# Queries of the cross attention as two 2x2x2 block products in seven multiplications

## The chip, the cores and the metric

The kernel runs on one core of a Trainium2 chip. The core has five engines, each with its own queue of instructions that it works through in order: TensorE (PE, matmuls and transposes; its weight loads are listed apart as PEld), VectorE (DVE), ScalarE (ACT), GpSimd (POOL) and SyncE (SP, which here only starts transfers). POOL starts the transfers that add to their destination ("accumulates"). Transfers between HBM (the `DRAM` of the code) and SBUF run beside the engines. The metric is the device time of one execution in microseconds (us). Three runs of the kernel before took 748.03 to 748.14 us, with a median of 748.14 us.

## The reference

One layer works on 512 tokens of width 1024. In its middle stands a cross attention with 4 heads of 256 onto 256 memory tokens:

```python
h = h + jnp.concatenate([fox_out, rec], axis=-1) @ w_out[l]
mem_n = rmsnorm(mem, norm_mem_g[l])
h = h + memory_cross_attention(rmsnorm(h, norm_x_g[l]), mem_n, w_xq[l], w_xkv[l], w_xo[l])
u = rmsnorm(h, norm_ff_g[l]) @ w1[l]
h = h + jnp.square(jax.nn.relu(u)) @ w2[l]

def memory_cross_attention(h, mem_n, w_q, w_kv, w_o):
    q = (h @ w_q).reshape(b_, s_, X_HEADS, X_HEAD_DIM)
    k, v = jnp.split(mem_n @ w_kv, 2, axis=-1)       # then split into heads
    s = jnp.einsum('bshd,bmhd->bhsm', q, k).astype(jnp.float32) / math.sqrt(X_HEAD_DIM)
    p = jax.nn.softmax(s, axis=-1)
    o = jnp.einsum('bhsm,bmhd->bshd', p.astype(v.dtype), v).reshape(b_, s_, D_MODEL)
    return o @ w_o
```

Before it stand an input projection, forgetting attention ("fox") and a gated recurrence; behind it the MLP with w1 and w2 and a final norm. All is in float32. The change concerns `q = h @ w_q`, a product of 512x1024 by 1024x1024.

## The kernel before

**Arithmetic.** A float32 product is made of three matmuls with operands of a reduced float32 type (`fp32r`): each operand is split into a high part and the rest, and hi*hi, lo*hi and hi*lo are summed in PSUM. For weights, ACT makes the high part (`wh..`, L184) and DVE the rest (`wl..`, L188), 128x1024 elements at a time. For activations, `x_hi` is made by ACT and `x_lo` by DVE.

**Stages around the change**, in the order of PE. The product with w_out (`wo`, `residual`, order k 4 to 7 and then 0 to 3) ends with, for each of eight row blocks, the sum into the residual `hT` (L1317, DVE), `x_hi` (L1318, ACT), `x_lo` (L1319, DVE) and two POOL instructions that sum squares (`wosq`, `ssq`). Then `x_proj(0)` makes the queries of head 0: one panel of w_xq, 256 columns in two loads of 512 KB, 48 matmuls of 128x512. The mean of squares (`pm`, `mean_sq`) and the reciprocal root on POOL follow. Then a loop over four heads: `x_scores` for two halves of the tokens (24 matmuls of 128x256 a head) and the softmax (maximum on DVE, exponential on ACT, division on DVE), `x_T_` (transposes `xpt`), the split of the transposed weights (`pth` on ACT, `ptl` on DVE) and `x_out` (12 matmuls of 128x512 a head, `xo`), whose results are split into `o_hi` and `o_lo`. Between these steps PE gets filling work from a list `fill`, in the amounts X1 to X4: beside head h the queries of head h+1, and beside head 3 the beginning of the product with w_xo (`xw`, `residual(...).early`). The rest of `xw` and the MLP come after.

**The weights' stream.** `specs` lists the panels in the order of their use, `next_panel` keeps two panels ahead: it starts the loads on SP and places the splits on ACT and DVE into the program, in its order. Where a split stands in an engine's queue is fixed when the program is built.

**The MLP's seven products.** The MLP is already computed by 2x2 blocks with seven block products in place of eight; matmuls are 128x256 there. It needs sums of weight blocks, which are made in DRAM: SP copies a block (L499) and POOL accumulates another one on it (L509). `Presum` gives one POOL accumulate to the program whenever PE has been given a certain amount of work (`PACE`: from 178 us on, one in 4.7 us, from 301 us on one in 11.5 us). One of the seven weights, "4" of the MLP, is made in SBUF: POOL accumulates a block onto the raw sum of another after that one has been split (L1528).

Of the kernel before, what the change touches and what calls it, by code (L numbers as in the profile page):

```python
# [9 lines left out]
F32 = mybir.dt.float32  # L10
# [6 lines left out]
P = 128  # L17
S = 512
# [28 lines left out]
def emit(  # L47
# [55 lines left out]
    def q2(name):  # L103
        return q2p.tile([P, S], R, tag="q2", name=name)
# [12 lines left out]
    def mm(name, shape=(S,)):  # L117
        return mmp.tile([P] + list(shape), F32, tag="mm", name=name)
# [43 lines left out]
    LATE = len(specs)  # L162
    for j in range(4):
        specs.append(panel(w_xkv, j * WT))
    for w in (w_out, w_xq, w_xo):
        for j in range(4):
            specs.append(panel(w, j * WT))
    NG = DFF // HG
    stream = []
    state = {"used": 0, "halves": 0}  # L170
# [93 lines left out]
    def product_unit(name):  # L264
# [24 lines left out]
            jobs.append(lambda: load_block("5", "10", raw0["5"]))  # L289
        return jobs  # L290

    def next_panel():
        while len(stream) < min(state["used"] + 2, len(specs)):
# [15 lines left out]
    def gemm_fm(ps, wt, col, ahi, alo, n=S, order=range(KC), begun=False):  # L309

        whi, wlo = wt
        sl = slice(col, col + P)
        for n_, k in enumerate(order):
            hi, lo = chunk(ahi, k, slice(0, n)), chunk(alo, k, slice(0, n))
            wh, wl = chunk(whi, k, sl), chunk(wlo, k, sl)
            te.matmul(ps, wh, hi, start=n_ == 0 and not begun, stop=False)  # L316
            te.matmul(ps, wh, lo, start=False, stop=False)  # L317
            at = te.matmul(ps, wl, hi, start=False, stop=k == order[-1])  # L318
            yield presum.tick(3 * n / 2400, at)
# [166 lines left out]
    def block2(g, rc):  # L486
        r, c = int(rc[0]), int(rc[1])
        k0 = g * HG + r * 2 * P
        return w2[k0 : k0 + 2 * P, c * S : (c + 1) * S].rearrange("(k p) n -> p k n", p=P)

    wsum = {}

    def sum_jobs(kind, g):
        block, shape = (block1, [P, UK, WT]) if kind == "u" else (block2, [P, 2, S])
        for name in SUMS:
            wsum[kind, g, name] = drp.tile(shape, F32, name=f"ws{kind}{g}{name}")

        def first(name):
            dma = nc.sync.dma_start(wsum[kind, g, name], block(g, SUMS[name][0]))  # L499
            copied.add((kind, g, name))  # L500
            return dma

        def sums():
            for name, (_, b) in SUMS.items():
                while (kind, g, name) not in copied:
                    copies.popleft()()
# [33 lines left out]
            return us  # L540

    presum = Presum()
    sets = []
    for g in range(DFF // HG):
        if g + 1 in SEVEN:
            sets.append(sum_jobs("u", g + 1))
# [744 lines left out]
    def residual(src_hi, src_lo, g, dst_hi, dst_lo, name, ssq, order, nlast, after=None, hooks={}, open_end=False):  # L1291

        ps_, gens = {}, {}

        def open_(c):
            if c % 2 == 0:
                open_.wt = next_panel()
            ps_[c] = mm(f"{name}{c}")
            gens[c] = gemm_fm(ps_[c], open_.wt, (c % 2) * P, src_hi, src_lo, order=order)

        def early():

            for c in range(3):
                open_(c)
                for _ in range(KC - nlast):
                    yield next(gens[c])

        def rest():
            for c in range(KC):
                if c not in gens:  # L1310
                    open_(c)
                yield from gens[c]
                if open_end and c == KC - 1:
                    last_xw.append(ps_[c])
                    return
                hc = hTc(c)
                ve.tensor_tensor(hc, hc, ps_[c], ALU.add)  # L1317
                ac.activation(dst_hi[:, c, :], hc, AF.Identity, scale=g[:, c : c + 1])  # L1318
                ve.scalar_tensor_tensor(dst_lo[:, c, :], hc, g[:, c : c + 1], f(dst_hi[:, c, :]), op0=ALU.mult, op1=ALU.subtract)  # L1319
# [12 lines left out]

        return early, rest
# [9 lines left out]

    x1_hi, x1_lo = act_tile("x1_hi"), act_tile("x1_lo")
    ssq1 = t2("ssq1")
    _, wo_rest = residual(mx_hi, mx_lo, g_x, x1_hi, x1_lo, "wo", ssq1, (4, 5, 6, 7, 0, 1, 2, 3), 1)
    run_now(wo_rest())


    o_hi, o_lo = act_tile("o_hi"), act_tile("o_lo")  # L1350
    x2 = []
    xq, xps, xpr, xpT = {}, {}, {}, {}

    def x_proj(h):
        wt = next_panel()
        xq[h] = []
        for i in range(2):
            ps = mm(f"xq{h}{i}")
            yield from gemm_fm(ps, wt, i * P, x1_hi, x1_lo)
            a, b = q2(f"xqh{h}{i}"), q2(f"xql{h}{i}")  # L1360
            ac.activation(a, ps, AF.Copy)
            ve.tensor_tensor(b, ps, f(a), ALU.subtract)
            xq[h].append((a, b))

    run_now(x_proj(0))
    ms1 = mean_sq(ssq1, "pm1")
    r1 = rstd_of(ms1, NT, "r1")
    gp.tensor_scalar(r16, r1, 1.0 / 16.0, 0.0, op0=ALU.mult, op1=ALU.add)

    def x_scores(h, tp):  # L1370
        ps = sc(f"xs{h}{tp}", (2, M))
        for j in range(2):
            ts_ = slice((2 * tp + j) * P, (2 * tp + j + 1) * P)
            for i in range(2):
                a, b = xq[h][i]
                kh_, kl_ = kTh[h][:, i, :], kTl[h][:, i, :]
                te.matmul(ps[:, j, :], a[:, ts_], kh_, start=i == 0, stop=False)
                te.matmul(ps[:, j, :], a[:, ts_], kl_, start=False, stop=False)
                te.matmul(ps[:, j, :], b[:, ts_], kh_, start=False, stop=i == 1)
# [12 lines left out]
        xpr[h, tp] = pr_  # L1392
# [38 lines left out]
                ve.tensor_copy(d, s_)  # L1431

    first_hooks, last_xw = {}, []
    fill.add(x_proj(1), "xq1")
    fill.run(2.0)
    for h in range(4):
        if 0 < h < 3:
            fill.add(x_proj(h + 1), f"xq{h + 1}")
        elif h == 3:
            x2_hi, x2_lo = act_tile("x2_hi"), act_tile("x2_lo")  # L1440
            early, rest = residual(o_hi, o_lo, g_ff, x2_hi, x2_lo, "xw", None, range(KC), 2, to_tok, first_hooks, True)
            fill.add(early())
        x_scores(h, 0)
        fill.run(X1)
        x_scores(h, 1)
        fill.run(X2 + X3)
        x_T_(h, 0)
        x_T_(h, 1)
        pth, ptl = s4([2, S], f"pth{h}", R), s4([2, S], f"ptl{h}", R)
        for mc in range(2):  # L1450
            ac.activation(pth[:, mc, :], xpT[h][mc], AF.Copy)
            ve.tensor_tensor(ptl[:, mc, :], xpT[h][mc], f(pth[:, mc, :]), ALU.subtract)
# [604 lines left out]
```

## Time and profile before

| | |
|---|---|
| median of three runs (range) | 748.14 us (748.03 to 748.14) |
| profiled execution, its own time | 748.24 us |
| span of the trace | 746.5 us |
| PE busy | 738.6 us (99%) |
| DVE, ACT, POOL busy | 566.6, 460.4, 213.4 us |
| product with w_out | 264.9 to 308.5 us of the span |
| cross attention from the first query matmul to the last of w_xo | 308.5 to 425.5 us |

Times in the trace count from the start of the span; what lies outside the span is 1.7 us. A row of a timeline has start, duration, engine, line and operation, output<-inputs; in brackets the idle time before it and what ended it. A matmul row's duration is modelled and overlaps the next one; what a matmul costs in a stream is the distance between two starts. Lines are those of the kernel before.

### The profile page before, as it was taken

To read this page: it belongs to the slowest core of one execution; us is meant where nothing else is said; L and a number is where in the kernel's file an instruction comes from. 1 tells how busy PE (TensorE), PEld (TensorE's weight loads), DVE (VectorE), ACT (ScalarE), POOL (GpSimd) and SP (SyncE) were. 2 spreads that over 40 slices of the span, in tenths; PEclk is the share of its full clock that TensorE was granted. 3 is DMA by queue.
4 is the path that set the end of the run, shared out by engine and by line. 5 is a ranking of instruction groups with operands and counts; after the bars stand their busy time and mean duration, and the time that the engine had idled before them with its cause. 6 is when DMAs were issued, how large, how long until landed. Compare 5 with 4: busy or idle time off the path is not lost.

```text
span 746.5 us, 12316 instructions
## 1 busy us (share of the span) xinstructions
PE 738.6 (99%) x4557; PEld 645.3 (86%) x4557; DVE 566.6 (76%) x892; ACT 460.4 (62%) x769; POOL 213.4 (29%) x290
## 2 busy tenths in 40 slices
PE   9999999999999999999999999999999999999996
PEld 6889888898888888888888899898989898999985
DVE  5878997677787866655546898978787878878796
ACT  5875876666666733244435589666665757574864
POOL 7216842442342246621012111111111111100034
PEclk9999999999999999999999999999999999999999
DMA  7797999857955899976669799898989899978352
GB/s 245 217 245 199 259 306 315 279 169 229 336 170 186 274 221 195 213 151 133 125 155 209 117 241 233 243 247 220 241 220 236 209 246 227 234 192 247 120 112 114
DMA packets 111918, 159.22 MB, mean 213 GB/s; under 512 B 6337, under 2 KB 74218, under 8 KB 111858
## 3 DMA queue, kind: packets, MB, share of 16 engines
q1 hardware_dynamic: 85490, 114.62, 46.6%
q0 software_dynamic: 26208, 43.54, 33.0%
q8 instruction: 36, 0.59, 0.3%
q10 hardware_dynamic: 160, 0.27, 0.1%
q14 instruction: 24, 0.20, 0.1%
HBM read 153.15 MB, written 51.40 MB: 274 GB/s over the span
## 4 chain that ended last, share of the span: by engine, by line
PE 90%; DMA 3%; DVE 2%; ACT 2%; issue 1%; POOL 0%; POOLq 0%; DVEq 0%; SPq 0%; ACTq 0%
PE uU L1632 4%; PE uU L1634 4%; PE uU L1633 4%; PE U L1790 3%; PE U L1791 3%; PE U L1792 3%; PE uY L1634 2%; PE uY L1633 2%; PE uY L1632 2%; PE xk L1146 2%; PE xq L316 2%; PE wo L316 2%; PE xq L317 2%; PE xq L318 2%; PE xw L318 2%; PE xw L317 2%
## 5 line engine op out<-in xcount | busy, mean ns | idle before, releaser
L188 DVE TENSOR_TENSOR wlu<-wru,whu 128x1024 fp32r<-128x1024 f32 x53 | 63.9, 1219 | 25.9 <-ACT whu L184 25.9
L184 ACT ACTIVATE whu<-wru 128x1024 fp32r<-128x1024 f32 x53 | 55.9, 1059 | 40.7 <-PE U L1792 16.8
L188 DVE TENSOR_TENSOR wld<-wrd,whd 128x1024 fp32r<-128x1024 f32 x56 | 68.2, 1220 | 13.9 <-ACT whd L184 13.7
L184 ACT ACTIVATE whd<-wrd 128x1024 fp32r<-128x1024 f32 x56 | 59.0, 1054 | 15.3 <-PE uU L1633 6.6
L1790 PE MATMUL U<-whd,hb 128*128 128x512 f32 x120 | 46.8, 390 | 0.0
L1791 PE MATMUL U<-wld,hb 128*128 128x512 f32 x120 | 46.8, 390 | 0.0
L1792 PE MATMUL U<-whd,hb 128*128 128x512 f32 x120 | 46.7, 389 | 0.0
L509 POOL DMA_DIRECT2D wsd<-in_w_dram x16 | 17.8, 1114 | 68.2 <-PE xw L318 16.6
L1167 POOL TENSOR_SCALAR bi<-nF,Ft 128x128 f32<-128x128 f32 (+3 forms) x32 | 20.8, 659 | 56.2 <-PE pt L1203 30.4
L1632 PE MATMUL uU<-xs_hi,whu 128*128 128x256 f32 x128 | 36.3, 284 | 0.0
L1634 PE MATMUL uU<-x_hi,wlu 128*128 128x256 f32 x128 | 36.2, 283 | 0.0
L1632 PE MATMUL uY<-xs_hi,whu 128*128 128x256 f32 x128 | 36.2, 283 | 0.0
L1633 PE MATMUL uY<-xs_lo,whu 128*128 128x256 f32 x128 | 36.2, 283 | 0.0
L1634 PE MATMUL uY<-xs_hi,wlu 128*128 128x256 f32 x128 | 36.2, 283 | 0.0
L1634 PE MATMUL uU<-xs_hi,wlu 128*128 128x256 f32 x128 | 36.2, 283 | 0.0
L1633 PE MATMUL uU<-x_lo,whu 128*128 128x256 f32 x128 | 36.2, 283 | 0.0
L1633 PE MATMUL uU<-xs_lo,whu 128*128 128x256 f32 x128 | 36.2, 283 | 0.0
L1632 PE MATMUL uU<-x_hi,whu 128*128 128x256 f32 x128 | 36.2, 283 | 0.0
L1528 POOL DMA_DIRECT2D wrd<-in_w_dram x8 | 9.8, 1223 | 86.6 <-DVE wld L188 51.4
L509 POOL DMA_DIRECT2D wsu<-in_w_dram x14 | 17.0, 1211 | 44.3 <-PE xq L318 14.5
L1318 ACT ACTIVATE x_hi<-hT,gv 128x512 fp32r<-128x512 f32 x15 | 10.7, 714 | 25.8 <-DVE hT L1317 25.8
L1792 PEld LDWEIGHTS U<-whd,hb 128*128 128x128 f32 x120 | 22.5, 188 | 4.7
(1012 smaller groups left out, 2656.4 us busy)
## 6 DMA issues: line engine op xcount, KB each, us to landing
wru<-in_w_dram SPq DMA_DIRECT2D x25, 512.0 KB, 6.7
wsd<-in_w_dram SPq DMA_DIRECT2D x24, 512.0 KB, 6.9
wrd<-in_w_dram SPq DMA_DIRECT2D x24, 512.0 KB, 4.2
wrd<-wsd SPq DMA_DIRECT2D x24, 512.0 KB, 5.7
wsu<-in_w_dram SPq DMA_DIRECT2D x21, 512.0 KB, 7.2
wru<-wsu SPq DMA_DIRECT2D x21, 512.0 KB, 5.5
wsd<-in_w_dram POOLq DMA_DIRECT2D x16, 512.0 KB, 8.0
wsu<-in_w_dram POOLq DMA_DIRECT2D x14, 512.0 KB, 7.6
```

The costliest lines, as they stand in the source:

```text
L184: at = ac.activation(hi, raw, AF.Copy)
L188: at_lo = ve.tensor_tensor(lo, raw, f(hi), ALU.subtract)
L316: te.matmul(ps, wh, hi, start=n_ == 0 and not begun, stop=False)
L317: te.matmul(ps, wh, lo, start=False, stop=False)
L318: at = te.matmul(ps, wl, hi, start=False, stop=k == order[-1])
L509: yield gp.dma_start(wsum[kind, g, name], src, accum_op=ALU.add, **more)
L1632: te.matmul(ps[:, i, :], whi[:, k, ws], xh[:, k, :], start=begin, stop=False, skip_group_check=True)
L1633: te.matmul(ps[:, i, :], whi[:, k, ws], xl[:, k, :], start=False, stop=False, skip_group_check=True)
L1634: at = te.matmul(ps[:, i, :], wlo[:, k, ws], xh[:, k, :], start=False, stop=k == UK - 1, skip_group_check=True)
L1790: te.matmul(ps, hi, whi[:, k, :], start=begin, stop=False, skip_group_check=True)
L1791: te.matmul(ps, hi, wlo[:, k, :], start=False, stop=False, skip_group_check=True)
L1792: at = te.matmul(ps, lo, whi[:, k, :], start=False, stop=k == 1, skip_group_check=True)
```

## The change

The columns of w_xq are taken in two groups of 512 (heads 0 and 1, heads 2 and 3), and each group as a product of 2x2 blocks of weights (halves of k, 256-column halves) with 2x2 blocks of x1 (halves of k, halves of tokens), in seven block products. A block product is 24 matmuls of 128x256; there are 14 of them. They are numbered `gn`, group and product. Three banks collect them: U, V and Y. V begins as a copy of U after product 1, Y becomes a copy of U after product 6 (its former content, product 5, is first saved as `y5`); products 7 and 3 end with a DVE sum with `y5` (`xt`), all outputs with a split.

- Weight sums "5", "7" and "6" of each group are made in DRAM, by 6 SP copies and 6 POOL accumulates, first in the list of `Presum`, whose pace begins at 150 us in place of 178. Weight "4" is made in SBUF: POOL accumulates block 10 onto the raw tile of "6" after that one's split.
- Token sums of x1 are made by ACT and DVE during the last blocks of `wo` and after its end (`x1_early`, `x1_sums`), in the rows of `o_hi` and `o_lo` that are still empty.
- Products 01, 11, 02, then `pm`, then 05, 06, 07, 04 run before the heads; 03, 15, 12, 16, 17, 14 and 13 fill the gaps of heads 0 and 1.
- Heads 2 and 3 are filled with `xw`: `early` first runs k 0 to 3 of three row blocks, then k 4 and 5.

```diff
-X1, X2, X3, X4 = 1.5, 2.0, 1.5, 2.0
+X1, X2, X3, X4, X5 = 1.5, 2.0, 1.5, 2.0, (3.0, 3.0)
+QN, NEED = 7, {1: "q03", 2: "q14", 3: "q13"}
-PACE = (178.0, 4.7), (301.0, 11.5)
+PACE = (150.0, 4.7), (301.0, 11.5)
...
+    QORDER = [(int(gn[0]), gn[1]) for gn in "01 11 02 05 06 07 04 03 15 12 16 17 14 13".split()]
...
+    def q_unit(g, name):
+        hi, lo = new_parts([UK, WT], f"q{g}{name}")
+        stream.append(([hi], [lo]))
+        if name == "4":
+            raw = q_raw.pop(g)
+        else:
...
+            if name in SUMS:
+                src = wsum["q", g, name]
+            else:
+                src = block_q(g, {"1": "00", "2": "10", "3": "11"}[name])
+            nc.sync.dma_start(raw, src)
+        if copies:
+            tc.keep_in_program_order(copies.popleft()())
+        jobs = [split_of(hi, lo, raw)]
+        if name == "6":
+            jobs.append(lambda: tc.keep_in_program_order(gp.dma_start(raw, block_q(g, "10"), accum_op=ALU.add)))
+        return jobs
...
-            for c in range(3):
-                open_(c)
-                for _ in range(KC - nlast):
-                    yield next(gens[c])
+            for ks in (range(UK), range(UK, KC - nlast)):
+                for c in range(3):
+                    if c not in gens:
+                        open_(c)
+                    for _ in ks:
+                        yield next(gens[c])
...
+    def x1_sums():
...
+        step(UK, h2, ALU.subtract)
+        parts("5", 1.0)
+        step(0, h1, ALU.add)
+        parts("6", -1.0)
+        hi, lo = x1s["7"]
+        for k in range(UK):
+            ac.activation(hi[:, k, :], d7[:, k, :], AF.Identity, scale=g_x[:, k : k + 1])
+        for k in range(UK):
+            ve.scalar_tensor_tensor(lo[:, k, :], d7[:, k, :], g_x[:, k : k + 1], f(hi[:, k, :]), op0=ALU.mult, op1=ALU.subtract)
+        step(UK, h1, ALU.subtract)
+        parts("3", -1.0)
...
+    def q_product(g, name):
+        b = {"5": "Y", "3": "Y", "2": "V"}.get(name, "U")
+        if (g, b) not in qbank:
+            qbank[g, b] = (pvt if (g, b) == (0, "Y") else mm)(f"xq{b}{g}").rearrange("p (i n) -> p i n", i=2)
+            if b == "V":
+                ac.activation(qbank[g, b], qbank[g, "U"], AF.Copy)
+        ps = qbank[g, b]
+        (whi,), (wlo,) = next_panel()
+        xh, xl = x1s[name]
+        for k in range(UK):
+            for i in range(2):
+                ws, begin = slice(i * P, (i + 1) * P), name in "15" and k == 0 and i == 0
+                te.matmul(ps[:, i, :], whi[:, k, ws], xh[:, k, :], start=begin, stop=False, skip_group_check=True)
+                te.matmul(ps[:, i, :], whi[:, k, ws], xl[:, k, :], start=False, stop=False, skip_group_check=True)
+                at = te.matmul(ps[:, i, :], wlo[:, k, ws], xh[:, k, :], start=False, stop=k == UK - 1, skip_group_check=True)
+            yield presum.tick(6 * WT / 2400, at)
...
+        elif name == "5":
+            y5s[g] = t2(f"xy5{g}", F32, (2, M))
+            ac.activation(y5s[g], ps, AF.Copy)
+        elif name == "6":
+            ac.activation(qbank[g, "Y"], ps, AF.Copy)
+        elif name in "73":
+            t = t2(f"xt{name}{g}", F32, (2, M))
+            ve.tensor_tensor(t, ps, y5s[g], ALU.add)
+            q_out(2 * g + 1, 1 if name == "7" else 0, t, -1.0)
...
-        if h < 3:
-            fill.until(f"xq{h + 1}")
-        else:
-            fill.run(X4)
+        fill.run(X4 if h > 1 else X5[h])
         x_out(h, pth, ptl)
```

**ACT from product 06's weights on.** In the names of the changed kernel, `whq_3707<-wrq_3709` is the split of "6" of group 0, `whq_3788<-wrq_3709` that of "4" from the same raw tile, `whq_3740` that of "7", `whq_3818` that of "3"; `xqV`, `xqU`, `xqY` are the banks.

```order
L189 ACTIVATE whq_3707<-wrq_3709 128x1024 [waits PE_49,Activation_49]
L1464 ACTIVATE xqV_3738<-xqU_3667 128x512 [waits PE_49]
L189 ACTIVATE whq_3740<-wrq_3742 128x1024 [waits DMAHW2_49,PE_49,Activation_49]
L1425 ACTIVATE o_hi<-xdif 128x1024 [waits DVE_49]
L1452 ACTIVATE xqh_3771<-xqV_3738 128x512 [waits PE_49,Activation_49]
L1481 ACTIVATE xy_3816<-xqY_3787 128x512 [waits PE_49]
L1425 ACTIVATE o_hi<-xdif 128x1024 [waits DVE_49]
L189 ACTIVATE whq_3788<-wrq_3709 128x1024 [waits DMASW7_49]
L189 ACTIVATE whq_3818<-wrq_3820 128x1024 [waits DMAHW3_49]
L1483 ACTIVATE xqY_3787<-xqU_3667 128x512 [waits PE_49,Activation_49]
```

The copy of U into Y (L1483) stands behind the splits of weights "4" and "3", and the split of "4" waits for a POOL transfer. In the kernel before, ACT's rows from the last sums of `wo` into the queries of head 0 (`xqh`, read from bank `xq`) read:

```order
L1318 ACTIVATE x_hi<-hT_3304,gv 128x512 [waits DMASW5_49,DVE_49]
L184 ACTIVATE wh30a<-wr30a 128x1024 [waits DMAHW0_49,PE_49,Activation_49]
L184 ACTIVATE wh30b<-wr30b 128x1024 [waits DMAHW1_49,PE_49]
L1318 ACTIVATE x_hi<-hT_3304,gv 128x512 [waits DVE_49]
L1361 ACTIVATE xqh_3654<-xq_3628 128x512 [waits PE_49]
L184 ACTIVATE wh31a<-wr31a 128x1024 [waits DMAHW2_49,PE_49,Activation_49]
```

The loads that these splits wait for are SP's, which wait for no instruction that is younger than the previous panel; no weight waits for a POOL transfer there.

**POOL in the changed kernel, from the last sum of squares of `wo` on.** `wrq_3709` is the raw tile of "6" again, the semaphore of DVE that it waits for is that of the split `wlq_3708`.

```order
L1371 TENSOR_TENSOR wosq_3636<-hT_3316 128x512 [waits DVE_49,Activation_49]
L1372 TENSOR_TENSOR ssq_3320<-ssq_3320,wosq_3636 128x512 [waits Pool_49]
L552 DMA wsd_210<-in_w_dram 256x1x512 [waits DMAHW6_49,PE_49]
L552 DMA wsu_208<-wsu_206 256x512 [waits DMASW6_49,DMAHW0_49,DMASW2_49,PE_49]
L326 DMA wrq_3709<-in_w_xq_dram 128x4x256 [waits DMASW7_49,DMAHW1_49,DVE_49,Activation_49]
L552 DMA wsd_211<-wsd_209 256x512 [waits DMASW3_49,DMASW0_49,PE_49]
```

The accumulate of block 10 (L326) is the transfer that the split of "4" waits for.

**DVE in the changed kernel, from the last residual sum of `wo` (`hT_3316<-hT_3316,wo_3607`) on**; `wlq_3676` is the split of "5", and that of "6", `wlq_3708`, is the next row behind the last one.

```order
L1362 TENSOR_TENSOR hT_3316<-hT_3316,wo_3607 128x512 [waits PE_49]
L1421 SCALAR_TENSOR_TENSOR xdif<-hT_3316,gv,xdif 128x256 [waits DVE_49]
L1439 SCALAR_TENSOR_TENSOR o_lo<-xdif_3476,gv,o_hi 128x256 [waits Activation_49]
L1364 SCALAR_TENSOR_TENSOR x_lo<-hT_3316,gv,x_hi 128x512 [waits Activation_49]
L1439 SCALAR_TENSOR_TENSOR o_lo<-xdif_3476,gv,o_hi 128x256
L1427 TENSOR_TENSOR o_lo<-xdif,o_hi 128x1024 [waits Activation_49]
L1439 SCALAR_TENSOR_TENSOR o_lo<-xdif_3476,gv,o_hi 128x256
L1421 SCALAR_TENSOR_TENSOR xdif<-hT_3310,gv,xdif 128x256 [waits DVE_49]
L1421 SCALAR_TENSOR_TENSOR xdif<-hT_3310,gv,xdif 128x256
L1421 SCALAR_TENSOR_TENSOR xdif<-hT_3312,gv,xdif 128x256 x2
L1439 SCALAR_TENSOR_TENSOR o_lo<-xdif_3476,gv,o_hi 128x256 [waits Activation_49]
L193 TENSOR_TENSOR wlq_3676<-wrq_3677,whq_3675 128x1024 [waits DMAHW1_49,Activation_49]
```

The token sums stand ahead of the weights' splits. (The next rows are the low part of token sum "6", 128x1024, and `wlq_3708`.)

**PE at head 3**: the last transposes, what stands before the first matmul with `pth` and `ptl`, and, further on, what follows the last of them. Before:

```order
L1400 MATMUL xpt_4253<-ident,xp_4229 128x128
L316 MATMUL xw_4245<-o_hi,wh33a 128x512
L317 MATMUL xw_4245<-o_lo,wh33a 128x512
L318 MATMUL xw_4245<-o_hi,wl33a 128x512
L316 MATMUL xw_4245<-o_hi,wh33a 128x512
L317 MATMUL xw_4245<-o_lo,wh33a 128x512
L318 MATMUL xw_4245<-o_hi,wl33a 128x512
L316 MATMUL xw_4245<-o_hi,wh33b 128x512
L317 MATMUL xw_4245<-o_lo,wh33b 128x512
L318 MATMUL xw_4245<-o_hi,wl33b 128x512
L1408 MATMUL xo_4277<-pth_4262,xvh_2289 128x512 [waits Activation_49]
L1409 MATMUL xo_4277<-ptl_4263,xvh_2289 128x512 [waits DVE_49]
```

After:

```order
L1530 MATMUL xpt_4537<-ident,xp_4514 128x128
L353 MATMUL xw_4441<-o_hi,wh44b 128x512
L354 MATMUL xw_4441<-o_lo,wh44b 128x512
L355 MATMUL xw_4441<-o_hi,wl44b 128x512
L1538 MATMUL xo_4555<-pth_4546,xvh_2295 128x512 [waits Activation_49]
L1539 MATMUL xo_4555<-ptl_4547,xvh_2295 128x512 [waits DVE_49]
```

Nine matmuls of `xw` stood between the transposes and `xo`, and now three do. Behind the twelve of `xo`, 21 matmuls of `xw` stood before the first that reads head 3's output, and now none does: the next is `xw_4362<-o_hi` with k 6.

More of the change, by code (lines that the diff above doesn't have):

```diff
@@ L164, in emit @@
         specs.append(panel(w_xkv, j * WT))
-    for w in (w_out, w_xq, w_xo):
-        for j in range(4):
-            specs.append(panel(w, j * WT))
+    for j in range(4):
+        specs.append(panel(w_out, j * WT))
+    QORDER = [(int(gn[0]), gn[1]) for gn in "01 11 02 05 06 07 04 03 15 12 16 17 14 13".split()]
+    QFIRST = len(specs)
+    specs += [lambda g=g, n=n: q_unit(g, n) for g, n in QORDER]
+    for j in range(4):
+        specs.append(panel(w_xo, j * WT))
     NG = DFF // HG
@@ L290, in product_unit, with parts_of @@
         return jobs
+    def parts_of(i):
+        return 1 if QFIRST <= i < QFIRST + len(QORDER) else 2
+    q_raw = {}
+    def q_unit(g, name):
[5 more added lines that the diff above has]
+            if name == "6":
+                raw = q_raw[g] = s4([UK, WT], f"wrq{g}{name}")
+            else:
+                state["halves"] += 1
+                if state["halves"] % 3 == 0:
+                    raw = t4(f"wrq{g}{name}")
+                else:
+                    raw = wrp.tile([P, D], F32, tag="wr", name=f"wrq{g}{name}", padded_shape=[P, UK * UW])
+                raw = raw.rearrange("p (k n) -> p k n", k=UK)
+            if name in SUMS:
+                src = wsum["q", g, name]
+            else:
+                src = block_q(g, {"1": "00", "2": "10", "3": "11"}[name])
[3 more added lines that the diff above has]
+        jobs = [split_of(hi, lo, raw)]
+        if name == "6":
+            jobs.append(lambda: tc.keep_in_program_order(gp.dma_start(raw, block_q(g, "10"), accum_op=ALU.add)))
+        return jobs
     def next_panel():
-        while len(stream) < min(state["used"] + 2, len(specs)):
+        while len(stream) < len(specs) and sum(parts_of(i) for i in range(state["used"], len(stream) + 1)) <= 4:
             for split in load_next():
@@ L542, in emit @@
     presum = Presum()
-    sets = []
+    sets = [sum_jobs("q", g) for g in range(2)]
     for g in range(DFF // HG):
@@ L1345, in emit, with x1_early @@
     ssq1 = t2("ssq1")
-    _, wo_rest = residual(mx_hi, mx_lo, g_x, x1_hi, x1_lo, "wo", ssq1, (4, 5, 6, 7, 0, 1, 2, 3), 1)
+    dif, dif7 = [], []
+    def x1_early():
+        dif.append(s4([UK, WT], "xdif"))
+        dif7.append(s4([UK, WT], "xdif7"))
+        for k in range(UK):
+            ac.activation(dif[0][:, k, :], hTc(k)[:, h2], AF.Identity, scale=g_x[:, k : k + 1])
+        for j in range(2):
+            ve.tensor_tensor(dif7[0][:, 2 * j : 2 * j + 2, :], hT[j][:, :, h1], hT[j][:, :, h2], ALU.subtract)
+    _, wo_rest = residual(mx_hi, mx_lo, g_x, x1_hi, x1_lo, "wo", ssq1, (4, 5, 6, 7, 0, 1, 2, 3), 1, hooks={3: x1_early})
     run_now(wo_rest())
@@ L1351, in emit @@
     x2 = []
[L1352 to L1365, printed above, removed]
+    xq, xps, xpr, xpT = {h: {} for h in range(4)}, {}, {}, {}
@@ new lines, in emit, with q_out, half @@
+    x1_sums()
+    qbank, y5s = {}, {}
+    def q_out(h, tp, src, sign):
+        def half(part):
+            name = f"xq{part}{h}{tp}"
+            return q2(name).rearrange("p (i n) -> p i n", i=2) if h % 2 == 0 else t2(name, R, (2, M))
+        a, b = half("h"), half("l")
+        ac.activation(a, src, AF.Copy, scale=sign)
+        if sign > 0:
+            ve.tensor_tensor(b, src, f(a), ALU.subtract)
+        else:
+            ve.scalar_tensor_tensor(b, src, sign, f(a), op0=ALU.mult, op1=ALU.subtract)
+        xq[h][tp] = a, b
@@ L1366, in emit @@
+    for g, name in QORDER[:3]:
+        run_now(q_product(g, name))
     ms1 = mean_sq(ssq1, "pm1")
```

51 lines of the change are left out of this document (40 added, 11 removed).

## Prediction

> **What bounds the kernel now.** I began with the page's busy times.
>
> ```profile
> span 746.5 us, 12316 instructions
> PE 738.6 (99%) x4557; PEld 645.3 (86%) x4557; DVE 566.6 (76%) x892; ACT 460.4 (62%) x769; POOL 213.4 (29%) x290
> L1167 POOL TENSOR_SCALAR bi<-nF,Ft 128x128 f32<-128x128 f32 (+3 forms) x32 | 20.8, 659 | 56.2 <-PE pt L1203 30.4
> ```
>
> PE works through the whole span, so a time can change in two ways only: PE gets less to do, or it has to wait. To see which holds around the change I took busy times by stretches: the product with w_out, the first queries, the first MLP products (the only ones of today that work in blocks of 256), and the end. Columns: stretch, length, then busy time and count for PE, PEld, DVE, ACT and POOL, the granted clock, the DMA share and GB/s.
>
> ```profile
> 264.90:308.50 43.60, 43.60 (x193) 36.10 (x193) 26.14 (x25) 13.14 (x17) 26.88 (x21) 1.00 0.93 194
> 308.50:323.10 14.60, 14.60 (x70) 12.08 (x68) 8.34 (x8) 4.85 (x6) 7.32 (x7) 1.00 1.03 219
> 425.50:446.00 20.50, 20.50 (x173) 20.46 (x172) 18.82 (x24) 17.25 (x29) 2.85 (x3) 1.00 0.87 232
> 740.50:744.00 3.50, 0.04 (x1) 0.00 (x0) 1.16 (x5) 1.20 (x3) 0.55 (x1) 1.00 0.56 219
> 744.00:745.00 1.00, 0.00 (x0) 0.00 (x0) 0.00 (x0) 0.00 (x0) 0.00 (x0) 0.66 0.75 281
> 745.00:746.50 1.50, 0.00 (x0) 0.00 (x0) 0.00 (x0) 0.00 (x0) 0.00 (x0) 0.50 0.00 0
> ```
>
> PE never waits in the first three. DVE has room (8.34 of 14.60 us in the stage that is replaced), the transfers hardly any.
>
> **What the change saves on PE.** The product with w_out has 192 matmuls of 128x512 in 43.6 us, 0.227 each, and the query product in place today has as many: 43.6. For 128x256 the timeline has the distance of two starts:
>
> ```profile
> 425.46 0.28 PE L1632 MATMUL uU<-x_hi,whu 128*128 128x256 f32 x1
> 425.58 0.28 PE L1633 MATMUL uU<-x_lo,whu 128*128 128x256 f32 x1
> ```
>
> That is 0.120, more than half of 0.227; the stretch from 425.5 says why, with PEld busy for 20.46 of 20.50 us: weight loads set the pace. 14x24 = 336 matmuls take 40.3 us, so seven products in place of eight give 3.3 us, not an eighth of 43.6. The Trainium skill, "TensorE: Matmul & The Clock Gate", section "Back-to-back issue gap", gives N/2.4+2.5 ns for an isolated gap and adds that weight loads belong into a stream's spacing; by its formula 512 and 256 columns would cost 216 and 109 ns and the gain would be 4.8. The trace disagrees for 256 (120 ns), and the row decides.
>
> **The wait before product 07.** I count from T, the end of `wo` on PE (308.5 in this trace). These rows give the prices around T: the last matmul of `wo` and the next, the residual sum, `x_hi`, a 128x1024 split on ACT and on DVE, `x_lo` beside POOL's squares, the means; then a 256-wide DVE instruction and ACT one, and the MLP's bank copy.
>
> ```profile
> 306.90 1.22 DVE L188 TENSOR_TENSOR wl30a<-wr30a,wh30a 128x1024 fp32r<-128x1024 f32 x1 [1.28 <-ACT wh30a L184]
> 308.48 1.06 ACT L184 ACTIVATE wh30b<-wr30b 128x1024 fp32r<-128x1024 f32 x1 [1.61 <-PE wo L317]
> 308.50 0.39 PE L316 MATMUL xq<-x_hi,wh29a 128*128 128x512 f32 x1
> 308.70 0.69 DVE L1317 TENSOR_TENSOR hT<-hT,wo 128x512 f32<-128x512 f32 x1 [0.58 <-PE wo L318]
> 309.44 0.71 ACT L1318 ACTIVATE x_hi<-hT,gv 128x512 fp32r<-128x512 f32 x1
> 311.58 1.78 DVE L1319 SCALAR_TENSOR_TENSOR x_lo<-hT,gv,x_hi 128x512 fp32r<-128x512 f32 x1
> 319.43 0.95 PE L1338 MATMUL pm<-ones,ssq 128*128 128x1 f32 x8
> 320.23 0.49 PE L316 MATMUL xq<-x_hi,wh30a 128*128 128x512 f32 x1
> ...
> L1153 DVE TENSOR_TENSOR kT<-xkt,kT x8: 404/416/422, 236.9 to 266.2; 128x256 fp32r<-128x256 f32 x8
> ...
> L1123 ACT ACTIVATE me<-mnt,gv 128x256 fp32r<-128x256 f32 x8 | 3.7, 463 | 0.5 <-PE mnt L1120 0.5
> ...
> L1647 ACT ACTIVATE uY<-uU x8: 582/582/582, 437.2 to 690.8; 128x512 f32<-128x512 f32 x8
> ```
>
> DVE, in the order shown above: the residual sum ends at T+0.89 (309.39). Behind it stand nine 256-wide instructions (9 x 0.42 = 3.8), `x_lo` (1.78, since POOL squares the same block), and four 128x1024 ones, the low parts of token sums 5 and 6 and of weights "5" and "6" (4 x 1.22 = 4.9). The low part of weight "6" is done at T+11.4. Then POOL issues the accumulate of block 10, at T+11.5. ACT keeps ahead of this: `x_hi` to T+1.65, token sum 5 1.06, a piece of 7 0.46, weights "5" and "6" 2.12, the copy of U into V 0.58, so that V is ready at T+5.9 and PE, there at T+5.8, loses about 0.3 with the signal's 0.2.
>
> What a POOL accumulate into SBUF takes from issue to landing stands in the MLP's rows for the same thing, first over all, then the first of the same shape (4x256):
>
> ```profile
> DMA to landing us min/median/max: 5.6/9.3/11.2
> ...
> wru<-in_w_dram POOLq DMA_DIRECT2D x1, 512.0 KB, 8.7
> ```
>
> I take 8.7: it is the one of the shape, among transfers at a share of 0.87, and the stretch here has 1.03. It lands at T+20.2. Only then ACT does the high part of "4" (1.06) and of "3" (1.06), and only behind them the copy of U into Y (0.58), which PE needs before 07 may overwrite U: T+20.2 + 0.1 + 2.7 + 0.2 = T+23.2. PE itself is done with 06 at: 01 and 11, 5.8; 0.3; 02, 2.9; `pm` 0.8; 05 and 06, 5.8; together T+15.5. It waits **7.7 us**. Ends: 5.6 us landing gives 4.6, 11.2 gives 10.2. If nothing stood ahead of it, the copy alone would cost 0.2 + 0.58 + 0.2 = 1.0.
>
> **The clock.** PE's last matmul begins at 740.26; the granted clock is 1.00 to 744, then 0.66 and 0.50, so it halves some 4 us after PE falls idle. A wait of 7.7 us is longer. The only cold start in the trace is the beginning:
>
> ```profile
> 1.29 3.17 PE L428 MATMUL warm<-zero 128*128 128x512 bf16 x7 [1.29 <-DVE ones L432]
> 740.26 0.28 PE L1827 MATMUL Z<-whd,hb 128*128 128x256 f32 x1
> ```
>
> Seven 512-wide matmuls take 3.17 us in place of 1.59. Estimate for a restart: 1.6 us; ends 0 (no drop) and 3.2 (twice as long). The same page of the Trainium skill, section "What's actually happening", says that one idle window of about 3.4 us halves the clock and one busy window restores it; by it the price is half a window, 1.7. The end of the trace agrees; no run here shows a drop in the middle.
>
> **Smaller waits on PE.** After 07, product 04 accumulates on U, which the DVE sum `xt` must have read: 0.2 + 0.69 + 0.1 = 1.0 us with nothing between; likewise 17 to 14, 1.0. The accumulate of group 1 has some 20 us of products and heads ahead of its use, and the U-to-Y copy there stands beside a score step of 12 matmuls (1.4 us against 1.0): both nothing. For head 3 the trace has the softmax chain:
>
> ```profile
> 381.85 0.48 PE L316 MATMUL xw<-o_hi,wh33a 128*128 128x512 f32 x1
> 382.02 1.09 ACT L1451 ACTIVATE pth<-xpt 128x512 fp32r<-128x512 f32 x2 [2.01 <-PE xpt L1400]
> 382.65 1.29 DVE L1452 TENSOR_TENSOR ptl<-xpt,pth 128x512 fp32r<-128x512 f32 x2 [1.79 <-ACT pth L1451]
> 383.99 0.39 PE L1408 MATMUL xo<-pth,xvh 128*128 128x512 f32 x1
> ```
>
> The first `ptl` half ends 1.45 us after the transposes (383.30). Nine matmuls covered that; the three left cover 0.7, and the second of `xo` comes 0.2 later: 0.65 us lost. The output rows 7 that `xw` reads straight behind `xo` need 0.2 + 0.58 + 0.69 + 0.2, less three matmuls of k 6 and one more (0.9): 0.6, ends 0 and 1.0. The covers of the other transposes stay at some 3.5 us: 15 matmuls of 512 or 30 of 256.
>
> **Moved work that I price at nothing.** Six POOL accumulates move into the stretch of the fox heads (1.1 us of issue each, 6.7 us): POOL's row L1167 on the page has 56.2 us of idle time before its 32 instructions, which hides them; without that cover PE would lose up to 6.7, and a gain has no mechanism, since PE is never idle there. SP carries six more copies and six more loads past 264 to 323; the load of raw "6", ahead of those of "1" on SP, waits for an accumulate that is issued beside the fox heads, before 262. If SP's cover is gone, a split is late by one landing; I keep 3 us for that in the upper end. The MLP's sums are issued at the same pace behind them, nothing.
>
> **Sum.** -3.3 + 0.3 + 7.7 + 1.6 + 2.0 + 0.65 + 0.6 = +9.55. The profiled execution took 748.24 (span 746.5 and 1.7 around it), 0.1 above the median of 748.14; from the median, **757.7 us**.
>
> **Rivals.** (a) A short wait: the accumulate lands like the fastest row, 5.6, and PE's wait of 4.6 keeps the clock up or nearly: -3.3 + 0.3 + 4.6 + 0.4 + 3.2 = +5.2, 753.3 us. For it: queue shares fall to 0.87 and less later; against it: 1.03 here. (b) Crowding: 6 more loads and 14 more DRAM passes where the share is 0.93 to 1.03, so that the accumulate lands at 11.2 or a load is late too: -3.3 + 0.3 + 10.2 + 1.7 + 3.2 = +12.1, 760.2, with a late split 763. (c) The POOL issues delay the fox heads, half uncovered: +3.4 on my sum, 761.1. (d) Faster: the copy of U into Y isn't held up, because the split of "4" is early. That needs the accumulate to land within 1 us of its issue; then the copy costs its own 1.0, and if the `xt` sums and head 3 are covered by what PE has queued, -3.3 + 0.3 + 1.0 = -2.0, 746.1 us. With them exposed it is +1.2, so even then the gain needs both. No row lands under 5.6. The case that the change doesn't do what it says, PE doing no less, differs by 3.3 only, and the weight-load row excludes it.
>
> **Numbers.** My forecast 0.55, own range 755.5 to 760; (a) 0.20; (b) 0.13; (c) 0.06; (d) 0.06, a third of it for exposures that leave the time within 0.2% of the median, about what a measurement of this kernel can tell from no change. Faster 0.04, same 0.02, slower 0.94. The range leaves out (d), the lower edge of (a) and the late split: 751.5 to 763.5, in which the two ends of the landing (4.6 and 10.2) and of the clock (0 and 3.2) lie.
>
> **What would show it.** The first matmul of 07 behind an idle PE of 5 to 10 us, released by ACT's copy L1483, itself behind the split of "4" that a POOL transfer releases; a granted clock under 1 in that stretch and matmuls of 07 at more than 0.120; 0.120 elsewhere in the products; about 1 us of idle before 04 and before 14, released by DVE L1486; 0.6 before the second matmul of head 3's `xo`; no idle PE up to the end of `wo`. I would be wrong if PE didn't idle before 07, or if the stages before T took longer.

## Result: slower by 2.1%, and the profile after

The changed kernel takes 764.71 us (median of five runs, 763.47 to 764.74) against 748.14 for the kernel before beside it; the ratio is 1.0212, with a 95% interval of 1.0201 to 1.0224. I had forecast 757.7 us and a range to 763.5: slower was right, but by 16.6 us and not by 9.6, and the time lies above the range. The profiled execution took 764.74 us.

The page of the changed kernel begins:

```profile
span 763.0 us, 12700 instructions
PE 742.7 (97%) x4701; PEld 653.8 (86%) x4701; DVE 585.3 (77%) x923; ACT 475.3 (62%) x792; POOL 221.2 (29%) x298
```

PE is 97% busy in place of 99%. The view of waits, for PE from 255 to 450 us, says where it stood still (tile and line that waited, what released it, total, times, longest):

```profile
PE xqU L1471 <- ACT xqY L1483: 4.9, 1, 4.9
PE xqV L1471 <- ACT xqV L1464: 3.8, 1, 3.8
PE xqU L1471 <- DVE xt L1486: 2.2, 2, 1.4
PE xpt L1530 <- DVE xp L1521: 0.8, 2, 0.4
PE xo L1539 <- DVE ptl L1580: 0.2, 1, 0.2
PE xw L354 <- DVE o_lo L1542: 0.2, 1, 0.2
```

The first row is the wait that I had forecast at 7.7 us, ahead of product 07. The second, ahead of 02, I had put at 0.3. All of the loss lies here: w_out ended at 309.0 in place of 308.5, the first MLP matmul began at 442.0 in place of 425.5, and the last matmul of the program at 756.8 in place of 740.3, so that the MLP kept the 16.5 us and added nothing.

Busy times by stretches: the beginning of w_out, the two waits, and product 02 and product 07 behind them (columns as in the prediction):

```profile
264.90:284.00 19.10, 19.10 (x90) 15.74 (x87) 12.12 (x13) 6.68 (x12) 9.06 (x8) 1.00 1.12 301
314.80:318.70 3.90, 0.13 (x2) 0.00 (x0) 3.90 (x4) 3.90 (x7) 3.11 (x3) 0.76 1.09 240
318.70:324.00 5.30, 5.29 (x27) 5.30 (x27) 5.30 (x10) 1.99 (x2) 0.89 (x1) 0.53 0.81 113
330.40:335.60 5.20, 0.26 (x4) 0.05 (x2) 1.74 (x4) 2.55 (x4) 1.44 (x3) 0.83 1.07 236
335.60:340.90 5.30, 5.30 (x24) 5.17 (x24) 2.12 (x2) 0.92 (x2) 0.00 (x0) 0.52 0.54 155
```

Both waits cost the clock: it is granted at 0.53 and 0.52 in the products behind them. A product that takes 24 x 0.120 = 2.9 us took 5.2 (318.70 to 323.85, and 335.59 to 340.8): 2.3 us each time. In the first wait ACT and DVE are busy for all of the 3.9 us, so they weren't waiting then; they had become late earlier. The chain that ended last, in order of time, says by what:

```profile
276.03 13.37 DMA wr28b<-in_w_out_dram
...
292.26 18.89 DMA wrq<-in_w_xq_dram
311.26 1.07 ACT whq L189
312.35 1.23 DVE wlq L193
313.58 0.61 DVE hT L1362
...
325.41 7.62 DMA wrq<-in_w_xq_dram
...
334.96 0.59 ACT xqY L1483
335.59 0.58 PE xqU L1471
```

A load of 512 KB for product 02 took 18.9 us. Its splits stand in the queues of ACT and DVE ahead of the last residual sum of w_out (`hT`, L1362), which needed nothing from that load: the sum begins at 313.5, some 4.3 us after PE had delivered its bank, and everything behind it on both engines, the token sums and the copy of U into V, moved by as much. The transfers' view shows that this load was no exception. First the loads of w_out and w_xq (L210) of the kernel before from 245 to 312 us, then those of the seven products from 270 to 345 (with POOL's accumulate of 7.6 us into one of their tiles among them):

```profile
DMA to landing us min/median/max: 3.5/5.3/7.3
```

```profile
DMA to landing us min/median/max: 4.8/13.9/18.9
```

What runs beside them is in the order of SP. In the kernel before, SP issues no copy for the MLP's weight sums after 262 us: the last one stands ahead of the load `wr27b` of w_out. In the changed kernel six follow behind that place, the last at 295 us, in between the loads of w_out and of the seven products. The copies for the new sums are first in a list that is worked off one by one beside the loads, and so the end of the list moved back by six.

### The profile page after: what moved, and what is told of

Same layout as the page of the kernel before. It is cut to its first block, busy times and chain, and to the rows that moved or that the text cites. A ratio compares the mean times of both kernels' runs of the same rounds, so it can differ in the third digit from the quotient of the medians.

```text
span 763.0 us, 12700 instructions
## 1 busy us (share of the span) xinstructions
PE 742.7 (97%) x4701; PEld 653.8 (86%) x4701; DVE 585.3 (77%) x923; ACT 475.3 (62%) x792; POOL 221.2 (29%) x298
## 4 chain that ended last, share of the span: by engine, by line
PE 77%; DMA 9%; DVE 7%; ACT 4%; issue 2%; POOL 0%; SPq 0%; POOLq 0%; DVEq 0%; ACTq 0%
PE uU L1757 4%; PE uU L1759 4%; PE uU L1758 4%; DMA wrq<-in_w_xq_dram 3%; PE U L1916 3%; PE U L1915 3%; PE U L1917 3%; PE uY L1759 2%; PE uY L1758 2%; PE uY L1757 2%; PE xk L1189 2%; DMA wr28b<-in_w_out_dram 2%; PE xw L354 2%; PE xw L355 2%; PE Y L1916 2%
## 5 line engine op out<-in xcount | busy, mean ns | idle before, releaser
L552 POOL DMA_DIRECT2D wsu<-in_w_dram x14 | 16.5, 1182 | 81.7 <-PE xw L355 22.6
L1653 POOL DMA_DIRECT2D wru<-in_w_dram x7 | 9.2, 1314 | 85.2 <-DVE wlu L193 85.2
L189 ACT ACTIVATE whq<-wrq 128x1024 fp32r<-128x1024 f32 x14 | 14.5, 1052 | 24.3 <-DMA wrq<-in_w_xq_dram 15.2
L193 DVE TENSOR_TENSOR wlq<-wrq,whq 128x1024 fp32r<-128x1024 f32 x14 | 17.0, 1221 | 15.9 <-ACT whq L189 15.9
```

What stands on the lines that cost most here:

```text
L189: at = ac.activation(hi, raw, AF.Copy)
L193: at_lo = ve.tensor_tensor(lo, raw, f(hi), ALU.subtract)
```

## Experiments

Two causes were to be told apart: the late loads (before 02), and ACT's order around the accumulate (before 07). Four kernels ran on one chip; the kernel before took 749.08 us there.

**The sums alone.** The kernel before with the six copies and six accumulates, unused.

```diff
-    sets = []
+    sets = [sum_jobs("q", g) for g in range(2)]
...
-PACE = (178.0, 4.7), (301.0, 11.5)
+PACE = (150.0, 4.7), (301.0, 11.5)
```

> The kernel before, with the six weight sums of w_xq made in DRAM as in the changed kernel (six SP copies and six POOL accumulates first in the lists, pace from 150 us) and not used for anything. Theory A (the sums push the MLP's copies in between the loads of w_out and w_xq, and these loads land late): loads of w_out and w_xq take over 11 us from issue to landing in place of 3.5 to 7.3, and the time rises by 0 to 3 us only, since these loads are some 10 us ahead of their use here. Rival B (the loads of the changed kernel are late because the units of the seven products need other buffers and stand behind loads that wait): the loads stay under 8 us and the time within 0.5 us of the kernel before.

It took 749.08 us, ratio 1.0003 (0.9993 to 1.0013): no change. Its loads of w_xq are late all the same, in the transfers' view from 255 to 325, and so is the DMA share of w_out's stretch:

```profile
wr29a<-in_w_xq_dram SPq DMA_DIRECT2D x1, 512.0 KB, 13.7
wr30b<-in_w_xq_dram SPq DMA_DIRECT2D x1, 512.0 KB, 12.9
```

```profile
264.90:308.50 43.60, 43.60 (x193) 36.08 (x194) 25.89 (x25) 13.12 (x16) 26.25 (x21) 1.00 1.12 285
```

So the traffic of the sums makes loads late by itself, if not as late as in the changed kernel: the slowest of all loads of w_out and w_xq from 245 to 330 us takes 13.7 us here and 18.9 there, and what makes the rest was not tried. PE waited for nothing in this run, so late loads cost nothing where their weights are used some ten microseconds later and nothing urgent stands behind the splits. It also excludes that the accumulates hold up the fox heads.

**No sums.** The changed kernel, with plain blocks in place of the DRAM sums.

```diff
-PACE = (150.0, 4.7), (301.0, 11.5)
+PACE = (178.0, 4.7), (301.0, 11.5)
...
-                src = wsum["q", g, name]
+                src = block_q(g, SUMS[name][0])
...
-    sets = [sum_jobs("q", g) for g in range(2)]
+    sets = []
```

> The changed kernel without the six DRAM sums (no copies, no accumulates for w_xq, pace from 178 us as before); weights 5, 6 and 7 are loaded as single blocks, so the queries are wrong. The accumulate of block 10 in SBUF stays. Theory A: the loads of 11 and 02 land in under 9 us, PE's wait before 02 falls from 3.9 to about 0.3 us and 02 runs at 0.120 a matmul; the wait before 07 grows from 5.1 to about 7.5, because PE is there earlier while the chain through the token sums is the same; about 760 us. Rival B: the wait before 02 stays at 3 to 4 us and the time at 764 to 765.

758.77 us, ratio 1.0129 (1.0112 to 1.0146). The wait before 02 is gone from the waits:

```profile
PE xqU L1471 <- ACT xqY L1483: 5.8, 1, 5.8
PE xqU L1471 <- DVE xt L1486: 2.0, 2, 1.2
```

The wait before 07 grew, as expected, but to 5.8 and not 7.5. Here the accumulate chain runs undisturbed, so its steps can be compared with the prediction's. T is 309.19. POOL's issue and ACT's split of "4":

```profile
321.34 1.33 POOL L326 DMA_DIRECT2D wrq<-in_w_xq_dram  x1 [3.60 <-DVE wlq L193]
...
327.84 2.00 ACT L189 ACTIVATE whq<-wrq 128x1024 fp32r<-128x1024 f32 x2 [4.37 <-DMA wrq<-in_w_xq_dram]
```

The issue is at T+12.2 (I had T+11.5), and 6.5 us lie to the split (I had 8.7).

**No accumulate.** The changed kernel without the accumulates of block 10.

```diff
-        if name == "6":
-            jobs.append(lambda: tc.keep_in_program_order(gp.dma_start(raw, block_q(g, "10"), accum_op=ALU.add)))
```

> The changed kernel without the two POOL accumulates of block 10 into SBUF, so weight 4 is wrong; all else stays. If the accumulate is what holds ACT's copy of U into Y: the wait before 07 falls from 5.1 to at most 1.2 us, 07 runs at 0.120 a matmul in place of 0.212 (2.3 us), the wait before 02 stays near 3.9; 757 to 759 us. Rival (late splits or token sums hold product 07 by themselves): the wait before 07 stays above 3 us and the time above 761.

758.82 us, ratio 1.0132 (1.0115 to 1.0148). The waits of PE:

```profile
PE xqV L1469 <- ACT xqV L1462: 3.7, 1, 3.7
PE xqU L1469 <- DVE xt L1484: 2.2, 2, 1.4
PE xqU L1469 <- ACT xqY L1481: 1.5, 1, 1.5
```

The wait before 07 falls to 1.5, a little more than the copy's own price, while the one before 02 stays; 07 runs at the full clock now (granted 1.00 from 331.3 to 334.3 us). (Since nothing is waited for, the scheduler also places the split of "4" further ahead on ACT.)

**Neither.** Both edits together.

> Both left out: no DRAM sums and no accumulate into SBUF (queries wrong). If the two causes add: both waits under 1.2 us, clock full throughout, 750 to 753 us; what is left above the kernel before, 2 to 5 us, is the small waits (before 04, before 14, the heads') less what PE saves. Rival (seven products in place of eight don't pay even then because of something else): above 755.

752.71 us, ratio 1.0047 (1.0032 to 1.0062). Against the changed kernel's 1.0212, each edit alone takes 0.8% off and both take 1.65%: the causes add.

```profile
PE xqU L1469 <- DVE xt L1484: 2.0, 2, 1.2
PE xqU L1469 <- ACT xqY L1481: 1.5, 1, 1.5
```

These two, with 0.7 for the transposes and twice 0.2 at head 3 by the same view, are 4.6 us of waits; against 3.3 saved on matmuls that leaves a loss of 1.3. The loss in this trace is larger: its first MLP matmul begins at 430.2, 4.8 us later than in the kernel before. The end of w_out, 0.8 us late, is another part, and the rest stays unassigned. So the seven products in this order lose even with both causes away.

**The copies moved.** The next three ran on another chip, where the kernel before took 748.79. The first is complete and issues the list's last thirteen copies, from the end of w_xkv's loads on, beside the loads of w_xo.

```diff
-COPIES = {12: 2, 19: 1, 20: 0, 24: 1}
+COPIES = {12: 2, 19: 1, 20: 0, 42: 2}
...
-        if copies:
-            tc.keep_in_program_order(copies.popleft()())
         jobs = [split_of(hi, lo, raw)]
```

> The changed kernel, complete, with one thing moved: the 13 last SP copies of the MLP's weight sums, which now stand between the loads of w_out and of the seven products, are issued beside the loads of w_xo instead. The POOL accumulates keep their pace, so the accumulates of w_xq beside the fox heads stay. If the SP copies are what made the loads late: loads of the seven products land in 5 to 9 us, no wait before 02, a wait before 07 of 5 to 8 us, 757.5 to 760 us, like the run without sums (758.8). If it is the POOL accumulates: loads stay at 12 to 19 us and the time at 763 to 765.

760.06 us, ratio 1.0155 (1.0139 to 1.0171), just above what I had put. The mechanism is as expected: the loads of the seven products from 262 to 340 land early again, but for the slowest, and no wait before 02 is left, with POOL's accumulates issued as they were.

```profile
DMA to landing us min/median/max: 3.5/5.7/9.9
```

```profile
PE xqU L1469 <- ACT xqY L1481: 5.9, 1, 5.9
PE xo L1537 <- DVE ptl L1578: 1.1, 2, 0.9
```

So the copies that SP issues, not POOL's accumulates alone, made the loads late; whether by their bytes or by their place between the loads was not told apart, and thirteen copies moved here, not only the six that had come in between. A wait of 0.9 us at head 0's `xo` is new; I didn't follow it.

**Reordered.** In addition another order of the products, and the split of "4" made dependent on the copy.

```diff
-    QORDER = ... "01 11 02 05 06 07 04 03 15 12 16 17 14 13"
+    QORDER = ... "01 11 02 05 06 12 07 03 04 15 16 17 13 14"
...
+        if name == "4":
+            def late(split=jobs[0]):
+                at = split("h")
+                if g in ycopy:
+                    tc.add_manual_dep(at.ins, ycopy[g].ins.name, order_, reason="ycopy")
+                split("l")
```

> The same with the products in the order 01 11 02 05 06 12 07 03 04, then 15 16 17 13 14 as filling, the split of weight 4 made to follow ACT's copy of U into Y, and shorter filling behind the transposes of heads 0 and 1 (1.8 in place of 3.0), so that one product's work stands between each copy or sum and its use. Complete computation. If the two waits and the half clock are the whole loss: no PE wait above 1 us between the end of w_out and the MLP, clock full, 746 to 750.5 us. If something else in the change costs time: 752 or more.

756.69 us, ratio 1.0111 (1.0095 to 1.0126): a miss. Two waits took the place of the old ones:

```profile
PE xqV L1479 <- ACT xqV L1472: 3.1, 1, 3.1
PE xpt L1538 <- DVE xp L1529: 2.1, 2, 1.0
```

Product 12 needs a third bank for group 1, which begins as a copy of U, and this copy stood on ACT behind a split that waited for PE until 324.5, a part of a token sum and the saving of `y5`. DVE had read the bank's former content by 324.0, so the wait was for ACT's queue. The products behind this wait run at half the clock again (granted 0.50 from 328 to 330 us). The transposes of heads 0 and 1 wait 1.0 us each for the softmax; whether the shorter filling or the new order does that was not tried.

**Matmuls in the waits.** The changed kernel with matmuls into an unused bank ahead of 02 and 07.

```diff
         (whi,), (wlo,) = next_panel()
+        if (g, name) in ((0, "2"), (0, "7")):
+            idle = sc(f"idle{name}")
+            for _ in range(16):
+                te.matmul(idle, x1_hi[:, 0, 0:P], x1_hi[:, 0, :], start=True, stop=True)
```

> The changed kernel, complete, with 16 matmuls of 128x512 (3.6 us) into an unused bank ahead of product 02 and 16 ahead of 07, that is within the waits of 3.9 and 5.1 us; the order on the other engines stays as it was. If the half clock of 02 and 07 comes from PE's idle time: both products run at 0.120 a matmul in place of 0.212; the 2.2 us gained by 02 go into a longer wait before 07, since DVE's chain sets that, and the 2.3 us of 07 are gained: 762 to 762.7. If the clock has another cause: 0.212 stays and the time is 764.5 or more.

763.9 us, ratio 1.0193 (1.0168 to 1.0218); by the medians it loses 15.1 us against the kernel before beside it, where the changed kernel lost 16.6, but the intervals overlap, so the total isn't shown to differ. The trace is plainer. Products 02 and 07 by stretches, and four starts in 07:

```profile
318.70:323.00 4.30, 4.30 (x38) 4.29 (x37) 4.30 (x9) 2.00 (x2) 0.00 (x0) 1.00 0.90 131
335.30:339.70 4.40, 4.32 (x24) 4.30 (x24) 0.80 (x1) 0.03 (x1) 0.00 (x0) 0.64 1.08 294
```

```profile
336.19 0.28 PE L1475 MATMUL xqU<-o_hi,whq 128*128 128x256 f32 x1
336.31 0.28 PE L1476 MATMUL xqU<-o_lo,whq 128*128 128x256 f32 x1
...
337.00 0.41 PE L1477 MATMUL xqU<-o_hi,wlq 128*128 128x256 f32 x1
337.21 0.41 PE L1475 MATMUL xqU<-o_hi,whq 128*128 128x256 f32 x1
```

With its wait filled, 02 runs at the full clock: the half clock of the changed kernel did come from PE's idle time. Before 07 a hole of 3.2 us was left, because PE got there earlier and DVE's chain did not; 07 begins at 0.12 a matmul and falls to 0.21 after 1.2 us. So the expected 2.3 us came only in part.

**Covered, and one swap.** Product 15 in place of 12 between 06 and 07, the bank of group 1's V from Y's pool, other fillings of the heads; and the same without the dependency, in which two instructions on ACT change places.

```diff
-X1, X2, X3, X4, X5 = 1.5, 2.0, 1.5, 2.0, (1.8, 1.8)
+X1, X2, X3, X4, X5 = (1.0, 0.6, 1.0, 1.0), 2.0, (1.8, 2.2, 1.5, 1.5), 1.3, (1.6, 1.6)
...
-    QORDER = ... "01 11 02 05 06 12 07 03 04 15 16 17 13 14"
+    QORDER = ... "01 11 02 05 06 15 07 03 04 12 16 17 13 14"
...
-            qbank[g, b] = (pvt if (g, b) == (0, "Y") else mm)...
+            qbank[g, b] = (pvt if (g, b) in ((0, "Y"), (1, "V")) else mm)...
```

> As the reordered run, with product 15 in place of 12 between 06 and 07 (the third bank's copy of group 1 had become a wait of 3.1 us there), that bank taken from the pool of Y, and the filling of the heads cut differently (less between the two score steps, more before the transposes). Complete computation. No PE wait above 1 us between w_out and the MLP, clock full, 746 to 751 us. If waits of 2 us or more stay at the heads, because DVE has fourteen weight splits and the token sums beside the softmax, 751 to 755.

> The same, except that two instructions on ACT change places: the split of weight 4, which waits for POOL's accumulate, stands ahead of the copy of U into Y, as in the changed kernel. Theory (ACT's order is what makes PE wait): the copy waits for the landing again; product 15 of 2.9 us stands between 06 and 07, so of the 5.8 us of the run without sums some 2 to 3.5 are left before 07, and the time is 2 to 4 us above the run beside it. If ACT's order doesn't matter: the same time within 0.7 us.

753.51 us, ratio 1.0068 (1.0055 to 1.0081), and without the dependency 753.63, ratio 1.0068 (1.0052 to 1.0083); before beside them 748.44. The covered order is the best complete version tried and still slower than the kernel before. The swap changed the time by 0.1 us where I expected 2 to 4. The covered order wasn't covered: the copy of U into Y holds PE twice in either run, before 07 and before 17. PE's waits in total and the first matmul of 07, with the dependency and without:

```profile
PE xqU L1479 <- ACT xqY L1491: 3.9, 2, 2.1
...
328.52 0.39 PE L1479 MATMUL xqU<-o_hi,whq 128*128 128x256 f32 x1 [1.78 <-ACT xqY L1491]
```

```profile
PE xqU L1469 <- ACT xqY L1481: 3.3, 2, 2.7
...
330.82 0.58 PE L1469 MATMUL xqU<-o_hi,whq 128*128 128x256 f32 x1 [2.65 <-ACT xqY L1481]
```

ACT around the copy, with the dependency and without:

```profile
325.36 1.06 ACT L189 ACTIVATE whq<-wrq 128x1024 fp32r<-128x1024 f32 x1 [6.64 <-DMA wrq<-in_w_xq_dram]
...
327.88 0.58 ACT L1491 ACTIVATE xqY<-xqU 128x512 f32<-128x512 f32 x1
```

```profile
329.23 1.06 ACT L189 ACTIVATE whq<-wrq 128x1024 fp32r<-128x1024 f32 x1 [1.49 <-DMA wrq<-in_w_xq_dram]
330.19 0.58 ACT L1481 ACTIVATE xqY<-xqU 128x512 f32<-128x512 f32 x1
```

With the dependency, another split, which waited 6.6 us for a load, holds ACT ahead of the copy; PE waits 1.8 us before 07, and the clock granted behind that is 0.55 from 328.5 to 332.0 us. Without it the copy waits for the split of "4", as forecast, and the wait before 07 is 2.65 us, within the 2 to 3.5 that I had put; but the run beside it was not free of waits, as I had assumed, and the wait before 17 falls from 2.1 to 0.7. So these two runs don't show what ACT's order alone is worth, and the waits of about 2 us of the covered run are the copy's, not the softmax's. In both orders one wait was swapped for another: some split ahead of the copies in ACT's queue waited for a load or an accumulate.

## Why the prediction was right and wrong, point by point

- **Seven products give 3.3 us, not an eighth.** Right. The products run at 0.120 a matmul where nothing holds them.
- **A wait before 07, because the copy into Y stands behind the split of "4".** Right in place and mechanism, as the run without accumulates shows. The size was off: 5.1 us between starts in the changed kernel and 5.8 by the waits where the chain is undisturbed, for 7.7. The term was the landing, 6.5 us for 8.7; of rows between 5.6 and 11.2 I had taken a single one.
- **0.3 us before product 02.** Wrong, and this is the step that failed, together with "Moved work that I price at nothing": I priced SP's six more copies and its additional loads at nothing and allowed 3 us for one late landing in the upper end only. (The additional loads are four and not six: SP starts 12 loads of query weights in place of 8, and the two others are POOL's accumulates.) I had looked at where the six copies are issued and not at what they push: six copies for the MLP moved in between the loads, these took up to 18.9 us in place of 7.3 at most, and the splits that wait for them stand ahead of the residual sum on DVE and of the copy into V on ACT. V was ready at T+9.6 in place of T+5.9. It cost 3.9 us before 02 and a drop of the clock, 2.3 us. Rival (b) names crowding, but puts it into the accumulate's landing, which was not late at all (7.6 us), and into one late split; the case I gave 0.13 was the nearer one, at 760 to 763.
- **The clock, 1.6 us.** The mechanism was right, the size was not: 2.3 us behind each wait, and there were two waits. That only an idle time of some 4 us lowers the clock did not hold either: the covered run has half the clock behind a wait of 1.8 us.
- **1.0 us each before 04 and 14.** Between starts 1.0 and 1.6; right but for 0.6 on the second.
- **Head 3: 0.65 and 0.6.** 0.5 each between starts, beyond what a matmul costs anyway. The two sums as they are written give 0.55 and 0.77, not 0.65 and 0.6; the total moves by less than 0.1. Two waits before transposes, together 1.2 us, I had called covered; their cover of 30 matmuls is some 0.5 us too short.
- **The six accumulates beside the fox heads at nothing.** Right, by the sums alone. The changed kernel ends w_out 0.5 us late all the same, and so does the run without sums (0.7), where the shift is there already at 152 us; what it comes from was not tried. In the covered run w_out ends at 308.4, so it is no fixed price of the change.

Summed with what was measured: -3.3 + 0.5 + 3.9 + 5.1 + 4.6 + 2.6 + 1.0 + 1.2 = +15.6 of 16.5; some 1 us stays unassigned. Rival (d) needed the waits to be hidden. Even without both causes the kernel was 0.47% slower, so the faster side was rightly given little.

## What to carry to other kernels

When work is put at the front of a list that is handed out one by one, price what it pushes: look up where the last items of the list are issued now, and what stands beside them. A late load cost nothing in the run of the sums alone, where only its own weights waited for it, and a lot in the changed kernel, where its split stood in an engine's queue ahead of an instruction on the critical chain; so check, for each split, what is next behind it. An algorithm that saves an eighth of the multiplications saved 3.3 us here, because a matmul of half the columns took 0.120 us and not half of 0.227, with the weight loads busy all the time, and each exposed copy or sum between dependent products (1.0 to 1.6 us) takes back a third to a half of that.

## What was unexpected of the hardware

- Six copies from DRAM to DRAM of 512 KB on SP's queue, beside loads of the same size and POOL's accumulates, went with more than double the loads' landing: median 13.9 us and up to 18.9, against 5.3 and 7.3, at a DMA share of 1.12 in place of 0.93. With thirteen copies moved away, these six among them, the median is 5.7 and the slowest 9.9.
- The clock can fall after PE has come back: behind a hole of 3.2 us, product 07 of the run with matmuls in the waits ran 1.2 us at 0.12 a matmul and then at 0.21. The Trainium skill, "TensorE: Matmul & The Clock Gate", section "What's actually happening", calls the window by which the clock is set free-running; a drop that comes after the hole agrees with that. In the changed kernel a wait of 3.9 us was enough for a product at half the clock, and in the covered run one of 1.8 us before 07 (granted 0.55 from 328.5 to 332.0 us), while one of 2.1 us before 17 in the same run cost none (1.00 from 350.9 to 354.0). So the length of a wait alone doesn't say whether the clock falls, and the 4 us and 3.4 us that the prediction went by are no safe limit.
